# Reordering the transfers of a scratch inverse, and five half-row moves, in the plan of a two-layer RWKV-7 / differential-attention trunk on one core

## The chip, the core and the metric

The kernel runs on one core of one Trainium2 chip. The metric is device time in microseconds of one execution. A core has five instruction streams that run in order and meet only at semaphores: TensorE (PE in the profile, its weight loads PEld), VectorE (DVE), ScalarE (ACT), GpSimd (POOL) and SyncE (SP), which here issues nearly all transfers; transfers are carried out by 16 DMA engines. The three runs of the kernel before took 1398.43 to 1399.07 us, with a median of 1398.93.

## What is computed

One inference step of a two-layer trunk, for a prompt of 512 tokens and a sample of 32 tokens, which the kernel treats as one matrix of 544 columns. Layer 0 is RWKV-7 time mixing, layer 1 differential attention; each has one input projection, cross attention to a memory, a SiLU gate, one output projection and a residual. The recurrence of layer 0, per head and token, is

```python
def step(S, inp):
    r_t, k_t, v_t, w_t, kk_t, a_t = inp
    sa = jnp.einsum('bhvk,bhk->bhv', S, -kk_t)
    S = (S * w_t[:, :, None, :] + sa[..., None] * (kk_t * a_t)[:, :, None, :]
         + v_t[..., None] * k_t[:, :, None, :])
    return S, jnp.einsum('bhvk,bhk->bhv', S, r_t)
...
y = (y - mean) * lax.rsqrt(var + GN_EPS) * ln_w + ln_b      # per head
y = y + jnp.sum(r * k * r_k, axis=-1, keepdims=True) * v
out = jnp.concatenate([y_mix, y_mem], axis=-1) * jax.nn.silu(gate)
return x + out @ w_out, S_T, last_row
```

There are 24 heads of 64; all matrices are float32.

## The kernel before

Layer 0 takes the heads two at a time: twelve *pairs*, each 128 partitions wide. The tokens are cut into eight chunks of 64, and the sample makes a ninth of 32. Inside a chunk the recurrence is solved as a triangular system, so a pair needs, for each of its chunks, small matrices (tile `at`, and `ats` for the sample) and the inverse of their triangular parts. The parts of the work on one pair are Python generators, and each step of one is a few instructions:

- `prep` (`rw_prep`, 33 steps) makes decays, keys and the small matrices of a pair, and near its end writes the triangular parts to a scratch in DRAM, `sc1` (the profile shows `sc<-at` x4 and `sc<-ats`).
- `inv` (`rw_invert`) reads `sc1` back in another layout into the tile `m` (`m<-sc` x6), and GpSimd eliminates: 31 times a product `tm<-u,m` (L867) and a sum `u<-u,tm` (L869).
- `back` (`rw_back`) writes the result `u` to another scratch, `sc2` (`sc<-u` x6), and `at` (`rw_at`) reads it from there into `at` and `ats` (`at<-sc` x4, `ats<-sc`).
- `mrg` (`rw_merge`) joins the two halves of the inverses: VectorE transposes (`t1b<-at`), TensorE multiplies (`ps_w`), ScalarE copies (`wm`, `at<-ps_w`).
- `val`, `chain` and `out` are the recurrence itself: nine chunks one after another (`ps_c`, `avz`, `sv`, `sd`, `SB`), then the outputs (`ps_yc`, `yt<-ps_yc`). `smp` is the sample's chunk and state.
- `fin` (`rw_finish`) is the norm of a pair's output: sums (`gs`), squares on ScalarE (`gsq`), `rsq`, a root by a chain of small VectorE instructions (`nt`, `q`), the product `yt<-yt,q`, transposes on TensorE (`ps_y`), and the gate.

The body of layer 0 is one loop over the pairs. Its turn for pair `pr` walks the 23 rows of the table `PLAN`: each row begins with one step of the chain of pair `pr`, and has two halves, each a list of steps (kind, pair relative to `pr`, and two costs in us that say how much TensorE and VectorE work the step is taken for). Between the steps matmuls of the main stream (`ps_g`, the projections) are laid, as many as the costs leave room for. While pair `pr` runs its chain, `prep` works on pairs `pr`+1 to `pr`+3, `inv` begins the inverse of pair `pr`+2, and `back`, `at` and `mrg` bring in the one of pair `pr`+1. Each engine's order is the program's order; no scheduler changes it.

The weights of the stream come in blocks: each block is loaded in two halves (`raw`, five buffers), two blocks ahead, split into a high part by ScalarE (`whi<-raw`) and a low part by VectorE (`wlo<-raw,whi`), and used in three products. The split's instructions, the gates and the token shift (`raw<-ps_g`, `shc`, `rkv<-raw`, `raw<-PC`, then VectorE's `rkv<-raw,PA,rkv`) are put off and let in one at a time at the end of a half row (`some`), where the costs have left room. Every transfer of this stretch is issued by SP, in program order, and SP stands at a transfer until what it waits for is there. Nearly every instruction goes through a recording helper, so its line is L106.

Of the kernel before, what the change touches and what calls it, by code (L numbers as in the profile page):

```python
# [47 lines left out]
FULL = ("full", 0, 0, 0)  # L48
PLAN = [
    [[("val", 0, 0.95, 0), ("prep", 2, 0.1, 0)], [("prep", 2, 0, 0.42)]],  # L50
    [[], [("prep", 2, 0, 1.04)]],
    [[("prep", 1, 0.53, 0)], [("prep", 1, 0, 0), ("prep", 2, 0.56, 1.0)]],
    [[("prep", 2, 0, 0)], [("prep", 2, 0, 1.0)]],
    [[("smp", 0, 0.11, 0.28), ("prep", 1, 0.4, 0)], [("prep", 2, 0, 0.86)]],
# [1 line left out]
    [[("prep", 2, 0, 1.1), ("smp", 0, 0.21, 0.29)], [("prep", 2, 0, 0.86)]],  # L56
    [[("prep", 2, 1.1, 1.37)], []],
    [[("smp", 0, 0.21, 0)], [("prep", 2, 0, 0.9)]],
    [[("prep", 2, 1.1, 1.37)], [("back", 1, 0, 0)]],
    [[("smp", 0, 0.6, 0.85)], []],  # L60
    [[("prep", 2, 0.5, 0.58)], [("at", 1, 0, 0), ("fin", -1, 0, 1.0)]],
    [[("prep", 2, 0.36, 0.43)], [("inv", 2, 0, 0), ("fin", -1, 0, 0.84)]],
    [[("prep", 2, 0.36, 0.43)], [("fin", -1, 0, 0), ("prep", 3, 0, 0)]],
    [[("prep", 2, 0.25, 0)], [("fin", -1, 0, 0.98)]],
    [[("prep", 2, 0.4, 0), ("smp", 0, 0.11, 0)], [("prep", 3, 0, 0.6)]],
    [[("prep", 3, 0.53, 0)], [("mrg", 1, 0, 0.86)]],
    [[("prep", 3, 0.11, 0.17), ("mrg", 1, 0.9, 0)], [("rsq", 0, 0, 1.5)]],
    [[("prep", 3, 0.33, 0)], [("fin", -1, 0, 0.88)]],
    [[("prep", 3, 0.33, 0)], [("prep", 3, 0, 0.1), ("fin", -1, 0.6, 1.0)]],
    [[("prep", 3, 0.33, 0)], [("mrg", 1, 0.9, 0), ("prep", 3, 0.33, 0), ("fin", -1, 0, 0.73)]],  # L70
    [[("prep", 3, 0, 1.45), ("val", 1, 0.45, 0)], [("prep", 3, 0, 0.5)]],
    [[("out", 0, 1.6, 0.7)], [("prep", 3, 0, 0)]]]
MEMPE = 4.8
SHIFTED, KEPT = 13, 24
LAM = 5
# [2173 lines left out]
```

## Time and profile before

| | before |
|---|---|
| median of 3 runs | 1398.93 us (1398.43 to 1399.07) |
| the profiled execution's own time | 1399.31 us |
| its span, first to last instruction | 1397.4 us |
| mean granted TensorE clock | 0.997 |
| TensorE busy | 1359.2 us (97%) |
| VectorE, ScalarE, GpSimd busy | 934.9, 827.4, 374.9 us |

The span is 1.9 us shorter than the execution's time; the rest lies around it. Busy times are sums over stages with different limits, so a stage is read by its own window; matmuls overlap, and a busy TensorE is one that has a matmul in flight. Rows of a timeline give start, duration, engine, line, operation and tiles, and in brackets the idle time of the engine before it and what ended that; "q" after an engine's name is its sequencer, which issues transfers. In names, an arrow separates what is written from what is read.

### The profile page before, as it was taken

To read this page: it belongs to the slowest core of one execution; us is meant where nothing else is said; L and a number is where in the kernel's file an instruction comes from. 1 tells how busy PE (TensorE), PEld (TensorE's weight loads), DVE (VectorE), ACT (ScalarE), POOL (GpSimd) and SP (SyncE) were. 2 spreads that over 40 slices of the span, in tenths; PEclk is the share of its full clock that TensorE was granted. 3 is DMA by queue.
4 is the path that set the end of the run, shared out by engine and by line. 5 is a ranking of instruction groups with operands and counts; after the bars stand their busy time and mean duration, and the time that the engine had idled before them with its cause. 6 is when DMAs were issued, how large, how long until landed. Compare 5 with 4: busy or idle time off the path is not lost.

```text
span 1397.4 us, 31954 instructions
## 1 busy us (share of the span) xinstructions
PE 1359.2 (97%) x11893; PEld 1295.8 (93%) x11893; DVE 934.9 (67%) x2345; ACT 827.4 (59%) x2304; POOL 374.9 (27%) x841
## 2 busy tenths in 40 slices
PE   8999999999999999999999999999999999999997
PEld 7988899999899998888899999999999999999997
DVE  5776778778877877676753477666466756767443
ACT  5766767867687777555543366664466546665222
POOL 2138557655775567510000040000000001001000
PEclk9999999999999999999999999999999999999999
DMA  6443222333223322342464473333333322332321
GB/s 221 149 129 83 62 59 64 91 89 76 69 77 84 77 68 69 96 119 74 128 189 130 118 217 100 92 97 90 99 92 99 99 73 84 101 105 82 91 76 72
DMA packets 264036, 139.45 MB, mean 100 GB/s; under 512 B 57721, under 2 KB 252802, under 8 KB 263882
## 3 DMA queue, kind: packets, MB, share of 16 engines
q1 hardware_dynamic: 263818, 137.41, 35.1%
q8 instruction: 94, 1.54, 0.5%
q14 instruction: 60, 0.49, 0.1%
q10 hardware_dynamic: 64, 0.02, 0.0%
HBM read 111.12 MB, written 22.91 MB: 96 GB/s over the span
## 4 chain that ended last, share of the span: by engine, by line
PE 82%; DVE 8%; ACT 5%; issue 2%; DMA 1%; POOL 1%; SPq 0%; DVEq 0%; POOLq 0%; ACTq 0%
PE ps_g L106 58%; PE ps_c L106 4%; PE ps_s L106 2%; PE ps_o L106 2%; PE ps_at L106 2%; DVE wlo L106 1%; PE ps_v L106 1%; PE ps_mo L106 1%; PE ps_mm L106 1%; PE ps_aT L106 1%; PE ps_w L106 1%; PE ps_yc L106 1%; PE ps_q L106 1%; PE ps_kv L106 1%; PE ps_mt L106 1%
## 5 line engine op out<-in xcount | busy, mean ns | idle before, releaser
L106 PE MATMUL ps_g<-hh,whi 128*128 128x272 f32 x1808 | 540.8, 300 | 0.4 <-DVE memk L106 0.2
L106 PE MATMUL ps_g<-hh,wlo 128*128 128x272 f32 x1808 | 536.0, 297 | 1.6 <-DVE wlo L106 1.6
L106 PE MATMUL ps_g<-hl,whi 128*128 128x272 f32 x1808 | 532.1, 295 | 0.6 <-DVE hl L106 0.3
L106 PEld LDWEIGHTS ps_g<-hh,wlo 128*128 128x128 f32 x1808 | 341.7, 189 | 6.3 <-DVE wlo L106 2.3
L106 PEld LDWEIGHTS ps_g<-hh,whi 128*128 128x128 f32 x1808 | 341.7, 189 | 5.7 <-DVE og L106 0.6
L106 PEld LDWEIGHTS ps_g<-hl,whi 128*128 128x128 f32 x1808 | 341.6, 189 | 4.6 <-DVE hl L106 1.3
L106 DVE TENSOR_TENSOR wlo<-raw,whi 128x512 fp32r<-128x512 f32 x314 | 220.1, 712 | 121.6 <-ACT whi L106 117.9
L106 ACT CAST whi<-raw 128x512 fp32r<-128x512 f32 x314 | 189.0, 619 | 107.8 <-PE ps_g L106 61.3
L867 POOL TENSOR_TENSOR tm<-u,m 102x84 f32<-102x84 f32 (+23 forms) x341 | 143.2, 420 | 165.7 <-DMA m<-sc 139.9
L869 POOL TENSOR_TENSOR u<-u,tm 102x84 f32<-102x84 f32 (+23 forms) x341 | 149.8, 439 | 26.6
L106 PE MATMUL ps_g<-hi,whi 128*128 128x272 f32 x512 | 149.0, 291 | 0.0
L106 PE MATMUL ps_g<-hi,wlo 128*128 128x272 f32 x512 | 147.6, 288 | 0.5 <-DVE wlo L106 0.5
L106 PE MATMUL ps_g<-lo,whi 128*128 128x272 f32 x512 | 147.5, 288 | 0.0
L1339 POOL TENSOR_TENSOR lo<-og,hi 128x544 fp32r<-128x544 f32 x8 | 13.2, 1652 | 359.9 <-ACT hi L106 359.4
L106 PEld LDWEIGHTS ps_g<-hi,wlo 128*128 128x128 f32 x512 | 96.5, 188 | 0.8 <-DVE wlo L106 0.7
L106 PEld LDWEIGHTS ps_g<-lo,whi 128*128 128x128 f32 x512 | 96.6, 189 | 0.0
L106 PEld LDWEIGHTS ps_g<-hi,whi 128*128 128x128 f32 x512 | 96.5, 189 | 0.0
L106 ACT ACTIVATE pt<-ps_s,snm 128x128 f32<-128x128 f32 (+3 forms) x96 | 50.9, 531 | 41.7 <-DVE snm L106 41.6
L106 DVE SCALAR_TENSOR_TENSOR SB<-ps_c,dl,sd 64x64 f32<-64x64 f32 x168 | 47.3, 282 | 38.9 <-PE ps_c L106 35.7
L1766 POOL TENSOR_TENSOR hl<-hn,hh 128x544 fp32r<-128x544 f32 x8 | 12.5, 1565 | 211.9 <-ACT hh L106 211.8
L106 ACT COPY sv<-ps_c 64x64 f32<-64x64 f32 x192 | 39.3, 205 | 33.0 <-PE ps_c L106 30.8
L106 ACT ACTIVATE sg<-ps_g 128x272 f32<-128x272 f32 x64 | 25.3, 395 | 54.5 <-PE ps_g L106 49.2
(402 smaller groups left out, 2580.6 us busy)
## 6 DMA issues: line engine op xcount, KB each, us to landing
raw<-in_rw_in_dram SPq DMA_DIRECT2D x114, 256.0 KB
raw<-in_df_in_dram SPq DMA_DIRECT2D x112, 256.0 KB
raw<-in_w_out_dram SPq DMA_DIRECT2D x64, 256.0 KB
oscr<-sg SPq DMA_DIRECT2D x16, 272.0 KB
lo<-oscr SPq DMA_DIRECT2D x16, 272.0 KB
m<-sc SPq DMA_DIRECT2D x33, 128.0 KB
raw<-in_w_mem_v_dram SPq DMA_DIRECT2D x16, 256.0 KB
kh<-kh SPq DMA_DIRECT2D x24, 136.0 KB
```

The source lines that it names most:

```text
L106: return lambda *a, **k: self.trunk.tie(self, issue(*a, **k))
L867: nc.gpsimd.tensor_tensor(tm[:, :n, :wd], u3[:, :n, kx : kx + 1].to_broadcast(sh), m3[:, kx : kx + 1, kx + 1 :].to_broadcast(sh), ALU.mult)
L869: nc.gpsimd.tensor_tensor(u3[:, :n, kx + 1 :], u3[:, :n, kx + 1 :], tm[:, :n, :wd], ALU.add)
L1339: (self.nc.gpsimd if g % 2 and self.o1 else self.ve).tensor_tensor(lo[:], t, hi[:].bitcast(F32), ALU.subtract)
L1766: nc.gpsimd.tensor_tensor(self.hl[:, k, :], h[:], self.hh[:, k, :].bitcast(F32), ALU.subtract)
```

## The change

The table `PLAN` is rewritten; nothing else is touched. `back` moves from row 9 to row 11 and `inv` from row 12 to row 11, behind it; `at` moves from row 11 to row 12. The writes of `sc1` belong to the `prep` step in the first half of row 11, which stays, so that the transfers of a turn now come in the order: next matrices written, results written, matrices read, results read. Five other steps move by half a row: `prep` of row 1 and `fin` of rows 13 and 18 to the first half, `prep` of row 15 to the second half, and `out` from the first half of row 22 to the second half of row 21.

```diff
-    [[], [("prep", 2, 0, 1.04)]],
+    [[("prep", 2, 0, 1.04)], []],
...
-    [[("prep", 2, 1.1, 1.37)], [("back", 1, 0, 0)]],
+    [[("prep", 2, 1.1, 1.37)], []],
     [[("smp", 0, 0.6, 0.85)], []],
-    [[("prep", 2, 0.5, 0.58)], [("at", 1, 0, 0), ("fin", -1, 0, 1.0)]],
-    [[("prep", 2, 0.36, 0.43)], [("inv", 2, 0, 0), ("fin", -1, 0, 0.84)]],
-    [[("prep", 2, 0.36, 0.43)], [("fin", -1, 0, 0), ("prep", 3, 0, 0)]],
+    [[("prep", 2, 0.5, 0.58)], [("fin", -1, 0, 1.0), ("back", 1, 0, 0), ("inv", 2, 0, 0)]],
+    [[("prep", 2, 0.36, 0.43), ("at", 1, 0, 0)], [("fin", -1, 0, 0.84)]],
+    [[("prep", 2, 0.36, 0.43), ("fin", -1, 0, 0)], [("prep", 3, 0, 0)]],
     [[("prep", 2, 0.25, 0)], [("fin", -1, 0, 0.98)]],
-    [[("prep", 2, 0.4, 0), ("smp", 0, 0.11, 0)], [("prep", 3, 0, 0.6)]],
+    [[("smp", 0, 0.11, 0)], [("prep", 2, 0.4, 0), ("prep", 3, 0, 0.6)]],
...
-    [[("prep", 3, 0.33, 0)], [("fin", -1, 0, 0.88)]],
+    [[("prep", 3, 0.33, 0), ("fin", -1, 0, 0.88)], []],
...
-    [[("prep", 3, 0, 1.45), ("val", 1, 0.45, 0)], [("prep", 3, 0, 0.5)]],
-    [[("out", 0, 1.6, 0.7)], [("prep", 3, 0, 0)]]]
+    [[("prep", 3, 0, 1.45), ("val", 1, 0.45, 0)], [("prep", 3, 0, 0.5), ("out", 0, 1.6, 0.7)]],
+    [[], [("prep", 3, 0, 0)]]]
```

On SP, in the turn of pair 3, where pair 4's results come back and pair 5's inverse begins, the rows before are these (`u_3747` is pair 4's result, `at_1695` and `sc_4458` are pair 5's matrices and their scratch, `at_90` is where pair 4's results go):

```order
 L106 DMA raw<-in_rw_in_dram 128x4x128 x2
 L106 DMA sc_4408<-u_3747 32x11x32 x2
 L106 DMA sc_4408<-u_3747 32x10x32
 L106 DMA sc_4409<-u_3747 2x11x32 x2
 L106 DMA sc_4409<-u_3747 2x10x32
 L106 DMA raw<-in_rw_in_dram 128x4x128 x2
 L106 DMA sc_4458<-at_1695 32x8x32 x4
 L106 DMA sc_4458<-ats 32x2x32
 L106 DMA at_90<-sc_4408 32x8x32 x4
 L106 DMA ats<-sc_4409 32x2x32
 L106 DMA m_4495<-sc_4458 32x1024
```

and now these (the names' numbers are new, the tiles the same):

```order
 L106 DMA raw<-in_rw_in_dram 128x4x128 x4
 L106 DMA sc_4450<-at_1695 32x8x32 x4
 L106 DMA sc_4450<-ats 32x2x32
 L106 DMA sc_4463<-u_3723 32x11x32 x2
 L106 DMA sc_4463<-u_3723 32x10x32
 L106 DMA sc_4464<-u_3723 2x11x32 x2
 L106 DMA sc_4464<-u_3723 2x10x32
 L106 DMA m_4471<-sc_4450 32x1024
...
 L106 DMA at_90<-sc_4463 32x8x32 x4
 L106 DMA ats<-sc_4464 32x2x32
```

Both weight loads and the writes of pair 5's matrices now stand ahead of the transfer that waits for GpSimd's result, and the reads of pair 4's results stand behind the six reads of pair 5's matrices.

On VectorE, in rows 16 to 18 of the same turn (merge, root and product of the norm), the rows before are:

```order
 L106 STREAM_TRANSPOSE t1b<-at_90 32x256 x2
 L106 TENSOR_TENSOR avz<-ps_c,avz 64x128
 L106 TENSOR_SCALAR q_99<-ps_s_4695 128x16
 L106 SCALAR_TENSOR_TENSOR rkv<-raw_485,PA,rkv 128x544
...
 L106 TENSOR_TENSOR wlo<-raw,whi 128x512
 L106 TENSOR_TENSOR yt_1689<-yt_1689,q_100 128x640
 L106 SCALAR_TENSOR_TENSOR SB_540<-ps_c,dl,sd 64x64 x2
 L106 TENSOR_TENSOR wlo<-raw,whi 128x512
```

and now:

```order
 L106 STREAM_TRANSPOSE t1b<-at_90 32x256 x2
 L106 SCALAR_TENSOR_TENSOR rkv<-raw_485,PA,rkv 128x544
 L106 TENSOR_TENSOR avz<-ps_c,avz 64x128
 L106 TENSOR_SCALAR q_99<-ps_s_4697 128x16
...
 L106 TENSOR_TENSOR yt_1689<-yt_1689,q_100 128x640
 L106 TENSOR_TENSOR wlo<-raw,whi 128x512
 L106 SCALAR_TENSOR_TENSOR SB_540<-ps_c,dl,sd 64x64 x2
```

The token shift's `rkv` moves ahead of `avz`, and the product `yt` ahead of the `wlo` that stood before it; the second `wlo` moves further down. The chain of the root, left out here, is the same in both.

On ScalarE, in rows 15 to 17 of that turn, the copies stood like this (`s_4674` is the copy that the transpose `ps_s` reads):

```order
 L106 COPY bt<-ps_bt 128x512
 L106 COPY so<-ps_so 64x64 x2
 L106 COPY raw_485<-ps_g 128x272
 L106 COPY s_4674<-ps_ss 128x128
 L106 COPY shc<-raw_485 128x2
 L106 ACTIVATE rkv<-raw_485,dv 128x544
 L106 COPY raw_485<-PC 128x1
```

and now stand like this:

```order
 L106 COPY so<-ps_so 64x64 x2
 L106 COPY raw_485<-ps_g 128x272
 L106 COPY bt<-ps_bt 128x512
 L106 COPY shc<-raw_485 128x2
 L106 ACTIVATE rkv<-raw_485,dv 128x544
 L106 COPY raw_485<-PC 128x1
 L106 COPY s_4678<-ps_ss 128x128
```

`bt` moves behind the evacuation of the main stream, and `s` behind the token shift's three instructions.

## The prediction

> **What bounds the kernel now.** I read the page's totals first, then a table by stage, then who waits for whom, then the timelines of one turn of the loop over head pairs.
>
> ```profile
> span 1397.4 us, 31954 instructions
> PE 1359.2 (97%) x11893; PEld 1295.8 (93%) x11893; DVE 934.9 (67%) x2345; ACT 827.4 (59%) x2304; POOL 374.9 (27%) x841
> 143.00:200.00 57.00, 54.58 (x544) 49.76 (x543) 43.08 (x108) 38.60 (x116) 35.80 (x87) 1.00 0.21 51
> 290.00:336.00 46.00, 45.14 (x470) 42.26 (x469) 36.62 (x91) 33.44 (x97) 29.23 (x65) 1.00 0.32 83
> 520.00:575.00 55.00, 50.25 (x526) 46.67 (x524) 43.84 (x115) 38.05 (x112) 30.05 (x70) 0.99 0.32 79
> ```
>
> The last three rows are stages of the pair loop (window, its length, busy time of PE, PEld, DVE, ACT, POOL). TensorE is the bound at full granted clock (1.00): in a middle turn it idles 46.00 - 45.14 = 0.86 us, in the first stage 2.42, in the one where the weight stream thins out 4.75. The edit leaves every TensorE instruction in place and only reorders them, so all that it can win is such idle time, and it loses only by making new. These waits end it:
>
> ```profile
> PE ps_y L106 <- DVE yt L106: 5.7, 9, 1.0
> PE ps_c L106 <- DVE avz L106: 2.4, 4, 1.4
> PE ps_w L106 <- DVE t1b L106: 2.1, 4, 1.1
> PE ps_ss L106 <- ACT bt L106: 0.8, 2, 0.6
>   PE ps_y L106: 5.0, 7
> ```
>
> (Four rows of the waits: total us, times, longest; the last is from the view of tile yt between 200 and 575 us.) The recurring one is ps_y, the transposes of the normalised output: seven waits, 5.0 us, one in each steady turn; two more, 0.7 us, come after 575.
>
> **The reordered transfers.** SP in the turn whose inverses are pair 4's (read back) and pair 5's (begun), and GpSimd beside it:
>
> ```profile
> 276.76 0.98 SPq L106 DMA_DIRECT2D raw<-in_rw_in_dram  x2
> 286.30 2.35 SPq L106 DMA_DIRECT2D sc<-u  x6
> 288.75 0.94 SPq L106 DMA_DIRECT2D raw<-in_rw_in_dram  x2
> 289.79 1.93 SPq L106 DMA_DIRECT2D sc<-at  x4
> 291.81 0.40 SPq L106 DMA_DIRECT2D sc<-ats  x1
> 292.31 1.85 SPq L106 DMA_DIRECT2D at<-sc  x4
> 294.75 2.04 SPq L106 DMA_DIRECT2D m<-sc  x6
> 286.04 0.23 POOL L869 TENSOR_TENSOR u<-u,tm 102x11 f32<-102x11 f32 x1
> 298.95 0.24 POOL L867 TENSOR_TENSOR tm<-u,m 102x31 f32<-102x31 f32 x1 [8.77 <-DMA m<-sc]
> SPq L106 <- POOL u L869: 68.5, 9, 10.2
> ```
>
> SP runs in order. It stands at the results' write (sc<-u) until the elimination ends (286.27): 68.5 us in nine turns, with the next weight load behind it. That load then goes out at 288.75, directly ahead of the matrices' writes (sc<-at). GpSimd starts 298.95 - (294.75 + 2.04) = 2.16 us after the last read of m was issued.
>
> In the new order both weight loads, then sc<-at and sc<-ats, come before anything that waits for GpSimd. What holds the chain then is VectorE's mask of the sample chunk:
>
> ```profile
> 282.18 0.67 DVE L106 TENSOR_TENSOR wlo<-raw,whi 128x512 fp32r<-128x512 f32 x1
> 284.65 1.29 DVE L106 TENSOR_TENSOR at<-ps_at,mk 128x512 f32<-128x512 f32 x2 [1.79 <-PE ps_at L106]
> 288.84 0.49 DVE L106 TENSOR_TENSOR ats<-ps_ats,mk 128x128 f32<-128x128 f32 x2
> 126.35 1.78 SPq L106 DMA_DIRECT2D at<-sc  x4
> 129.10 0.43 DVE L106 STREAM_TRANSPOSE t1b<-at 32x256 f32<-32x256 f32 x1 [0.60 <-DMA at<-sc]
> ```
>
> The second load needs a fifth raw buffer, free at 282.85 when that wlo ends; at is complete at 285.94, so the four sc<-at go out at 286; ats is complete at 289.33. Then, with the rows' durations and 0.1 us between kinds: sc<-ats to 289.8; six sc<-u to 292.2 (GpSimd was done at 286.3, so SP does not stand); six m<-sc to 294.3; four at<-sc to 296.2. GpSimd starts at 294.3 + 2.16 = 296.5, which is 2.5 us earlier. That gains nothing by itself, since no row above has TensorE waiting for GpSimd. The price is on the results: before they were issued by 294.16, now by 296.2. The first turn shows a released reader 129.10 - (126.35 + 1.78) = 0.97 us after the last issue; behind m's reads I bound it by m's own 2.16. So at lands between 297.2 and 298.4. Who waits:
>
> ```profile
> 297.87 0.58 DVE L106 SCALAR_TENSOR_TENSOR SB<-ps_c,dl,sd 64x64 f32<-64x64 f32 x2 [1.83 <-PE ps_c L106]
> 298.37 0.89 DVE L106 STREAM_TRANSPOSE t1b<-at 32x256 f32<-32x256 f32 x2
> 299.74 0.29 DVE L106 TENSOR_TENSOR avz<-ps_c,avz 64x128 f32<-64x128 f32 x1 [0.48 <-PE ps_c L106]
> 300.27 0.79 DVE L106 SCALAR_TENSOR_TENSOR rkv<-raw,PA,rkv 128x544 f32<-128x544 f32 x1
> 302.91 0.77 DVE L106 TENSOR_TENSOR wlo<-raw,whi 128x512 fp32r<-128x512 f32 x1
> 303.60 0.89 DVE L106 TENSOR_TENSOR yt<-yt,q 128x640 f32<-128x640 f32 x1
> 299.74 0.69 PE L106 MATMUL ps_w<-t1b,at 32*32 32x32 f32 x32
> 304.64 0.63 PE L106 MATMUL ps_y<-ident,yt 128*128 128x128 f32 x4 [0.68 <-DVE yt L106]
> L106 SPq DMA_DIRECT2D at<-sc x48: 307/441/1572, 126.4 to 607.9; - x48
> ```
>
> t1b, the merge's transpose, starts at 298.37, held by TensorE's ps_c, not by data: the results arrive 0 to 1.2 us ahead of it. If they are late, avz, the root chain and yt queue behind t1b on VectorE; ps_w has 299.74 - 299.26 = 0.48 us of cover. I take no stall in a normal turn, and +1.0 us in all for turns where one issue on SP is slow: the last row (min, median, max ns) has an issue of 1.57 against 0.44, 1.13 more, of which 0.5 is covered; one or two of nine turns. Bounds 0 and, with every turn late, the rival below.
>
> The Trainium skill, "DMA: Bandwidth & Descriptors", section "Anatomy of one DMA", fits a DMA (on GpSimd's path) as about 2.0 us fixed plus its bytes; from the issue of the last 32 KB read (296.2 - 0.44) that would be an estimated landing at 297.8, so no allowance, and a sum 1.0 us lower. The first turn's row gives 0.97 + 0.44 = 1.4 us for the same kind of read with nothing ahead of it, so here the rows are the shorter and decide.
>
> **The five moved half steps.** (1) `fin` in row 18: the multiply yt now stands before one wlo (0.77) instead of behind it, and rkv (0.79) moves ahead of avz, into the 0.48 us that VectorE idled there. So yt starts 0.7 (start to start, 303.60 - 302.91) plus about 0.4 earlier, 302.5 for 303.60, and ends at 303.4; TensorE reaches ps_y at 304.64 - 0.68 = 303.96. The longest ps_y wait is 1.0, less than the 1.1 won. Take all: -5.0 - 0.7 = **-5.7**. Bound: 0, if rkv itself waits. The second wlo, now behind avz, delays nothing that a row shows waiting.
>
> (2) `prep` in row 1: zr goes ahead of rkv. Where this mattered:
>
> ```profile
> 542.80 0.58 DVE L106 TENSOR_SCALAR SB<-ps_c,dl 64x64 f32<-64x64 f32 x2 [1.39 <-PE ps_c L106]
> 544.55 0.79 DVE L106 SCALAR_TENSOR_TENSOR rkv<-raw,PA,rkv 128x544 f32<-128x544 f32 x1 [1.17 <-ACT raw L106]
> 545.25 1.11 DVE L106 TENSOR_TENSOR zr<-rkv,de 128x512 f32<-128x512 f32 x2
> 546.40 0.28 DVE L106 TENSOR_TENSOR avz<-ps_c,avz 64x128 f32<-64x128 f32 x1
> ```
>
> VectorE idles 1.17 us before rkv, and avz behind it costs TensorE the 1.4 us wait. zr (1.11) fits into that gap: **-1.1**, bounds 0 and -1.4.
>
> (3) `prep` in row 15 and `fin` in row 13 reorder ScalarE: bt goes behind the output copies (so) and the evacuation, and s moves behind shc, rkv and raw:
>
> ```profile
> 298.27 0.28 ACT L106 COPY s<-ps_ss 128x128 f32<-128x128 f32 x1
> 299.32 0.19 ACT L106 COPY raw<-PC 128x1 f32<-128x1 f32 x1
> 299.54 0.27 PE L106 MATMUL ps_s<-ident,s 128*128 128x128 f32 x1
> ```
>
> s, last of the same copies, ends about where raw ended, 299.51, instead of 298.55, and ps_s wants it at 299.54: the cover of 1.0 us is used up. gsq, now ahead of an evacuation that ScalarE waited for, should win some back. **+0.5** for eight turns, bounds 0 and +4 (0.5 us each). (4) `out` in row 21: ps_yc and seven ps_g change places; the same matmuls, nothing.
>
> Sum, from the profiled execution's 1399.31: -5.7 - 1.1 + 1.0 + 0.5 = -5.3, 1394.0. That execution is 0.38 above the median of the runs (1398.93), so **1393.6**.
>
> **The rivals.** A, *the results come too late.* They now queue behind the reads of m. Landing 1.6 us after t1b's turn, with 0.5 covered, costs nine turns x 1.1 = 9.9 us at ps_w, in place of the allowance: 1393.6 - 1.0 + 9.9 = 1402.5. It is slower than before by 0.2% from (5.3 + 1.0 + 2.8) / 9 = 1.0 us a turn, that is reads landing 1.5 us behind t1b's turn, at 299.9, 3.7 us after their last issue. Against it: 0.97 and 2.16 in the rows. For it: margins of about half a microsecond, and one weight load that would still have to clear the queue if its buffer came later than 282.85. The same page, section "Latency and other measured facts", has a loaded memory access at up to 2 us against 0.2; by that rule A would come true if m's reads load the memory enough. No row here shows a read that late.
>
> B, *the won time is eaten.* ps_s waits 0.5 a turn for s (+4.0 instead of +0.5) and zr wins nothing: 1393.6 + 3.5 + 1.1 = 1398.2. For it: the cover of s shrinks from 1.0 to about 0. Against it: ScalarE is 59% busy, and idles close by.
>
> C, *more than ps_y goes.* The stages 143 to 200 and 520 to 575 idle 2.4 and 4.75 us with VectorE's and ScalarE's backlog ending most waits; if about 4 more of these 7 vanish, since bt no longer sits ahead of ps_ss and VectorE catches up: 1389.5.
>
> D, *the writes do not move* (the second load waits for a later wlo): then the reordering is idle, and (1) to (3) stand: as forecast, and counted there.
>
> **How the numbers follow.** Forecast 0.55, B 0.23, A 0.12, C 0.10. A measurement of this kernel tells about 0.2%, 2.8 us, from no change: 1396.1 and 1401.7. Faster: 0.50 of the forecast and C, 0.60. Within: the forecast's 0.05, B, a little of A, 0.29. Slower: A, 0.11. The forecast's own range is 1391.5 to 1396.5; for 8 in 10 it must take in B and half of C: 1389.0 to 1400.0.
>
> **What would show it.** Right: ps_y gone from the waits; GpSimd's first tm 2 to 3 us earlier against t1b; SP without a wait for u. Wrong: ps_w waiting for t1b in every turn, with t1b waiting for at<-sc (A); a new row ps_s for ACT s (B); ps_y still there with yt started late because rkv waited for raw.

## The result and the profile after

The changed kernel takes 1384.87 us (median of four runs, 1382.06 to 1385.84) against 1399.0 for the kernel before: a ratio of 0.9895, with a 95% interval of 0.9878 to 0.9912. It is 14.1 us faster, 2.7 times the 5.3 us of the forecast's sum, and lies below the predicted range (1389.0 to 1400.0). The traces compared below are of executions of 1399.31 and 1382.06 us, so the one of after is 2.8 us below its median, and the traces show 17 us where the medians differ by 14.

The page of the changed kernel begins:

```profile
span 1380.3 us, 31985 instructions
PE 1352.6 (98%) x11893; PEld 1292.9 (94%) x11893; DVE 931.4 (67%) x2345; ACT 828.0 (60%) x2304; POOL 384.7 (28%) x841
```

TensorE has the same 11893 matmuls, and is busy 6.6 us less with them. For the steady part I cut both traces at the end of VectorE's mask of the sample chunk (`ats`), from pair 3's mask to pair 11's, eight turns. First the window of the kernel before, then, of the changed one, the same eight turns, its first stage, one middle turn and the last stage (length, then busy time of PE, PEld, DVE, ACT, POOL):

```profile
197.46:562.78 365.32, 356.02 (x3694) 332.35 (x3693) 290.35 (x722) 263.69 (x762) 232.34 (x513) 1.00 0.30 78
```

```profile
196.49:549.62 353.13, 351.27 (x3694) 331.87 (x3693) 286.45 (x723) 264.28 (x762) 240.06 (x512) 1.00 0.31 78
...
143.00:200.00 57.00, 54.94 (x547) 50.30 (x546) 42.86 (x110) 39.32 (x118) 36.94 (x87) 1.00 0.26 62
285.30:329.84 44.54, 44.54 (x469) 42.16 (x468) 35.82 (x92) 33.40 (x96) 30.93 (x64) 1.00 0.31 79
520.00:575.00 55.00, 52.03 (x583) 48.10 (x582) 40.51 (x105) 37.18 (x108) 39.62 (x92) 1.00 0.27 73
```

Eight turns with the same 3694 matmuls take 353.13 instead of 365.32 us, 45.7 a turn before and 44.1 now. Of these 12.2 us the idle time gives 9.30 - 1.86 = 7.4, and 4.8 come out of time that was shown as busy. In the middle turn TensorE has no idle time left at all. Four of the waits that end TensorE's idle time are now (total us, times, longest; before, their totals were 1.5, 2.1, 5.7 and 2.4):

```profile
PE ps_c L106 <- ACT yt L106: 2.3, 6, 0.6
PE ps_w L106 <- DVE t1b L106: 1.1, 3, 0.6
PE ps_y L106 <- DVE yt L106: 0.7, 2, 0.4
PE ps_c L106 <- DVE avz L106: 0.3, 1, 0.3
```

The seven waits of the steady turns at ps_y are gone; the two late ones (0.7) are still there. Of the four waits behind avz one is left: the 1.4 us one is down to 0.3. The waits behind ScalarE's yt grew a little. In the changed kernel, SP and GpSimd in the turn that the prediction showed:

```profile
282.15 1.81 SPq L106 DMA_DIRECT2D sc<-at  x4
285.33 0.30 SPq L106 DMA_DIRECT2D sc<-ats  x1
285.73 2.38 SPq L106 DMA_DIRECT2D sc<-u  x6
288.16 2.41 SPq L106 DMA_DIRECT2D m<-sc  x6
290.67 1.79 SPq L106 DMA_DIRECT2D at<-sc  x4
```

```profile
281.02 0.23 POOL L869 TENSOR_TENSOR u<-u,tm 102x11 f32<-102x11 f32 x1
281.20 1.34 POOL L787 TENSOR_TENSOR rkk<-rkv 128x544 f32<-128x544 f32 x1
292.48 0.24 POOL L867 TENSOR_TENSOR tm<-u,m 102x31 f32<-102x31 f32 x1 [2.48 <-DMA m<-sc]
```

The elimination ends at 281.25 and SP asks for its result only at 285.73: SP no longer waits for GpSimd's result, but for VectorE's mask. VectorE, a little later in the turn:

```profile
293.79 0.58 DVE L106 SCALAR_TENSOR_TENSOR SB<-ps_c,dl,sd 64x64 f32<-64x64 f32 x2 [1.61 <-PE ps_c L106]
294.28 0.89 DVE L106 STREAM_TRANSPOSE t1b<-at 32x256 f32<-32x256 f32 x2
295.22 0.79 DVE L106 SCALAR_TENSOR_TENSOR rkv<-raw,PA,rkv 128x544 f32<-128x544 f32 x1
296.04 0.29 DVE L106 TENSOR_TENSOR avz<-ps_c,avz 64x128 f32<-64x128 f32 x1
...
298.67 0.83 DVE L106 TENSOR_TENSOR yt<-yt,q 128x640 f32<-128x640 f32 x1
```

There is no wait in front of t1b: the results, whose last read was issued by 292.46, were there. GpSimd's first tm starts 1.8 us ahead of t1b, where it was 0.6 behind it: 2.4 us earlier, as forecast (2.5). And rkv, avz, the root and yt follow without a gap.

### The profile page after: what moved, and what is told of

The parts are those of the page before. It is cut to its first block, busy times and chain, and to the rows that moved or that the text cites. A ratio compares the mean times of both kernels' runs of the same rounds, so it can differ in the third digit from the quotient of the medians.

```text
span 1380.3 us, 31985 instructions
## 1 busy us (share of the span) xinstructions
PE 1352.6 (98%) x11893; PEld 1292.9 (94%) x11893; DVE 931.4 (67%) x2345; ACT 828.0 (60%) x2304; POOL 384.7 (28%) x841
## 4 chain that ended last, share of the span: by engine, by line
PE 88%; DVE 6%; ACT 3%; issue 1%; DMA 1%; SPq 0%; DVEq 0%; ACTq 0%
PE ps_g L106 62%; PE ps_c L106 5%; PE ps_s L106 2%; PE ps_o L106 2%; PE ps_at L106 2%; PE ps_v L106 2%; PE ps_mo L106 1%; PE ps_mm L106 1%; PE ps_w L106 1%; PE ps_wa L106 1%; DVE wlo L106 1%; PE ps_aT L106 1%; PE ps_yc L106 1%; PE ps_kv L106 1%; PE ps_q L106 1%
## 5 line engine op out<-in xcount | busy, mean ns | idle before, releaser
L867 POOL TENSOR_TENSOR tm<-u,m 102x84 f32<-102x84 f32 (+23 forms) x341 | 146.1, 429 | 100.6 <-DMA m<-sc 71.7
L869 POOL TENSOR_TENSOR u<-u,tm 102x84 f32<-102x84 f32 (+23 forms) x341 | 155.8, 457 | 26.6
```

What stands on the lines that cost most here:

```text
L867: nc.gpsimd.tensor_tensor(tm[:, :n, :wd], u3[:, :n, kx : kx + 1].to_broadcast(sh), m3[:, kx : kx + 1, kx + 1 :].to_broadcast(sh), ALU.mult)
L869: nc.gpsimd.tensor_tensor(u3[:, :n, kx + 1 :], u3[:, :n, kx + 1 :], tm[:, :n, :wd], ALU.add)
```

## The experiments

The kernel before was timed beside each group of four: 1398.58, 1398.62 and 1399.19 us. Differences are taken against the one beside, or against the 1384.87 of the changed kernel, whose four runs (1382.06 to 1385.84) belong to none of these groups; so a difference of a microsecond or two against it is rough.

**The two halves of the change.** First the transfers alone:

```diff
-    [[("prep", 2, 1.1, 1.37)], [("back", 1, 0, 0)]],
+    [[("prep", 2, 1.1, 1.37)], []],
...
-    [[("prep", 2, 0.5, 0.58)], [("at", 1, 0, 0), ("fin", -1, 0, 1.0)]],
-    [[("prep", 2, 0.36, 0.43)], [("inv", 2, 0, 0), ("fin", -1, 0, 0.84)]],
+    [[("prep", 2, 0.5, 0.58)], [("fin", -1, 0, 1.0), ("back", 1, 0, 0), ("inv", 2, 0, 0)]],
+    [[("prep", 2, 0.36, 0.43), ("at", 1, 0, 0)], [("fin", -1, 0, 0.84)]],
```

> The three transfer steps alone (the five half-row moves undone). Theory S (the stops): TensorE never waited for GpSimd or for SP, so the order of the transfers is worth nothing to it; 1399 us, within 1 us of the kernel before, though SP's waits for GpSimd's result vanish and GpSimd starts about 2.5 us earlier. Rival T (the transfers): with SP no longer standing at the results' write, weight halves and inverses arrive earlier, the backlog on VectorE and ScalarE shrinks and several small stops with it: 1391 to 1394 us, a third to a half of the 14.1 us.

Measured: 1397.35 us, a ratio of 0.9992 (0.9984 to 1.0001): 1.2 us, not told apart from nothing. That is theory S but for 0.2 us, and rival T falls; SP's waits for GpSimd's result went away and next to nothing came of it.

Then the five half-row moves alone, with the transfers in their old places:

```diff
-    [[], [("prep", 2, 0, 1.04)]],
+    [[("prep", 2, 0, 1.04)], []],
...
-    [[("prep", 2, 0.36, 0.43)], [("fin", -1, 0, 0), ("prep", 3, 0, 0)]],
+    [[("prep", 2, 0.36, 0.43), ("fin", -1, 0, 0)], [("prep", 3, 0, 0)]],
...
-    [[("prep", 2, 0.4, 0), ("smp", 0, 0.11, 0)], [("prep", 3, 0, 0.6)]],
+    [[("smp", 0, 0.11, 0)], [("prep", 2, 0.4, 0), ("prep", 3, 0, 0.6)]],
...
-    [[("prep", 3, 0.33, 0)], [("fin", -1, 0, 0.88)]],
+    [[("prep", 3, 0.33, 0), ("fin", -1, 0, 0.88)], []],
...
-    [[("out", 0, 1.6, 0.7)], [("prep", 3, 0, 0)]]]
+    [[], [("prep", 3, 0, 0)]]]
```

(`out` goes to the end of the row above.)

> The five half-row moves alone, transfers in their old order. Theory S: all of the gain is here, 1385 us (within 1.5). Rival T: 1390 to 1393 us, since what the transfers bring is missing. If the two only work together, 1395 or more.

Measured: 1400.19 us, 1.0008 (0.9999 to 1.0016). Theory S falls, and T with it; the third case of the expectation holds, that the two only work together: the halves give -1.2 and +1.6 and together -14.1. The trace, of its fastest run (1397.54 us), says why. Its waits, and its eight turns in the same cut as above:

```profile
PE ps_q L106 <- POOL rkk L787: 13.8, 8, 2.7
...
PE ps_y L106 <- DVE yt L106: 0.4, 1, 0.4
PE ps_c L106 <- DVE avz L106: 0.3, 1, 0.3
```

```profile
196.73:563.15 366.42, 352.71 (x3694) 332.25 (x3693) 290.54 (x722) 264.70 (x762) 235.64 (x508) 1.00 0.30 77
```

The stops at ps_y and avz are gone as in the changed kernel, and TensorE's busy time is nearly that of the changed kernel (352.71 and 351.27). But the eight turns are as long as before, with 13.7 us of idle time, and a wait that was not there takes it: ps_q, for GpSimd's product rkk. GpSimd forms rkk right behind the elimination. In the kernel before, GpSimd in the turn of the prediction and around the next elimination, and then TensorE's use of the first rkk:

```profile
286.23 1.36 POOL L787 TENSOR_TENSOR rkk<-rkv 128x544 f32<-128x544 f32 x1
...
330.78 0.23 POOL L869 TENSOR_TENSOR u<-u,tm 102x11 f32<-102x11 f32 x1
330.97 1.34 POOL L787 TENSOR_TENSOR rkk<-rkv 128x544 f32<-128x544 f32 x1
344.63 0.24 POOL L867 TENSOR_TENSOR tm<-u,m 102x31 f32<-102x31 f32 x1 [9.27 <-DMA m<-sc]
```

```profile
289.50 0.62 PE L106 MATMUL ps_q<-rkk,hb 128*128 128x272 f32 x2
```

rkk is ready at 287.59, and TensorE takes it at 289.50: no wait, with 1.9 us to spare. But GpSimd has a loop of its own with SP: the elimination (298.95 to 331.01, 32.1 us), then results written, next matrices written, results read, next matrices read and landed (13.6 us, of which SP stands 1.5 for TensorE's ps_g), then the next elimination at 344.63. That is 45.68 us, and TensorE's turn was 45.71 (289.33 to 335.04). Single turns scatter, from 44.4 to 46.9 us between the starts of eliminations, so that this pair of turns agrees so closely is in part chance; over seven turns the means are 45.54 (209.73 to 528.49) and, from ps_q to ps_q, 45.61 (243.78 to 563.06). GpSimd was the second bound, just below the first. Take TensorE's stops away alone, and GpSimd's loop sets the turn; shorten that loop alone, and TensorE does.

The margin from rkk's end to ps_q, over the nine turns, says the same. It is 0.05 us in the first turn and 1.7 to 4.1 in the others in the kernel before, 3.5 to 6.4 with the transfers alone, 0.05 in every turn with the five moves alone, and 1.9 to 3.2 in the changed kernel. With the five moves alone the loop even became longer, 46.42 us a turn (209.18 to 534.14): its eight eliminations took 32.65 us on the mean, against 31.95 in the kernel before.

**The largest term alone.** The product yt ahead of one wlo, nothing else:

```diff
-    [[("prep", 3, 0.33, 0)], [("fin", -1, 0, 0.88)]],
+    [[("prep", 3, 0.33, 0), ("fin", -1, 0, 0.88)], []],
```

> Only the step fin of row 18 moved: yt ahead of one wlo on VectorE, TensorE's order unchanged. Counted from start to start of TensorE's matmuls, not by shown idle time, ps_y costs 6.8 us less after the change than before, where the idle rows say 5.0. Theory S: this move takes nearly all of that, 1392.2 us (within 1.5), and the ps_y waits fall from 5.7 to about 1. By the prediction on record, with idle time as the measure and rkv ahead of avz counted in: at most 5.7, 1393.3. Rival U (the product is early only if the steps before it are early too: rkv and the root's chain come ahead through the other moves): half of it, 1395 to 1397 us, with ps_y waits of 2 to 4 us left.

Measured: 1399.79 us, 1.0003 (0.9994 to 1.0013), with runs from 1395.60 to 1401.95. Its waits:

```profile
PE ps_q L106 <- POOL rkk L787: 4.6, 7, 1.3
...
PE ps_y L106 <- DVE yt L106: 0.4, 1, 0.4
```

The move takes ps_y's waits away, 5.7 to 0.4 us, more than S asked, and the time is unchanged: seven waits for rkk come in their place. All three expectations miss, since none had the stall go to GpSimd.

**`out` alone.**

```diff
-    [[("prep", 3, 0, 1.45), ("val", 1, 0.45, 0)], [("prep", 3, 0, 0.5)]],
-    [[("out", 0, 1.6, 0.7)], [("prep", 3, 0, 0)]]]
+    [[("prep", 3, 0, 1.45), ("val", 1, 0.45, 0)], [("prep", 3, 0, 0.5), ("out", 0, 1.6, 0.7)]],
+    [[], [("prep", 3, 0, 0)]]]
```

> Only the step out moved from row 22 to row 21. The prediction on record says nothing, 1399 us: the same matmuls in another order. Rival V: the move shifts where the token shift, the splits and the evacuations fall on ScalarE and VectorE for the whole turn behind it, and so takes the hidden stops at ps_c behind avz (4.4 us less from start to start after the change) and at the sample's transposes (so, si: 2.3 us less): 1392 to 1395 us.

Measured: 1395.7 us, 0.9982 (0.9973 to 0.9990): 2.9 us faster. So the move that I costed at nothing is worth something, as rival V says, a little less than it asks, and mostly not at its places: from the start of one matmul to the start of the next, ps_c behind avz costs 0.5 us more than before, and what falls is spread over ps_g (-1.2), si (-0.9, which V named), ps_c behind SB (-0.7) and smaller ones.

**The loop theory, tested on the two together.** The transfers and `fin` of row 18 (the diffs of the first and third experiment together):

> The three transfer steps and fin of row 18, the other four moves undone. Theory L (two loops): with fin of row 18 alone ps_y gave back 7.1 us from start to start, and 6.5 came back as ps_q's waits for GpSimd's rkk, because GpSimd's own loop through SP (elimination 32, then 13.3 us until the next matrices are read) was as long as a turn; the transfers alone gave 1.2. Where the transfers break that loop, the 7.1 stay: 1398.6 - 7.1 - 1.2 = 1390.3 us (within 1.5), ps_q's waits for rkk 0. Rival M (only the whole set of moves works): 1395 us or more, with the stops elsewhere, not at ps_q.

Measured: 1394.7 us, 0.9974 (0.9965 to 0.9983). No wait for rkk is left, as L says, and the transfers now let the move pay; but it pays 2.7 us beyond the transfers alone and not 7. Against the kernel before, ps_y's starts come 5.8 us cheaper; ps_c behind SB costs 2.2 more, and avz 0.5. The wlo that yt overtook still stands ahead of SB on VectorE, so SB comes no earlier, and TensorE, now sooner at the matmul that needs it, waits there: nearly half of the stop moved on to what was late next. That reading rests on VectorE's order and the start times. L's 1390.3 misses; M's 1395 or more is met but for 0.3 us, and the stops are elsewhere, as it says, not at ps_q.

**What breaks the loop.** The five moves again, with the matrices read ahead of the results, and the writes where they were before:

```diff
-    [[("prep", 2, 0.5, 0.58)], [("at", 1, 0, 0), ("fin", -1, 0, 1.0)]],
-    [[("prep", 2, 0.36, 0.43)], [("inv", 2, 0, 0), ("fin", -1, 0, 0.84)]],
+    [[("prep", 2, 0.5, 0.58)], [("inv", 2, 0, 0), ("at", 1, 0, 0), ("fin", -1, 0, 1.0)]],
+    [[("prep", 2, 0.36, 0.43)], [("fin", -1, 0, 0.84)]],
```

(against the five moves alone)

> The five moves with the writes in their old places, SP standing at the results' write as before; only inv is put ahead of at, so that the next matrices are read before the results. Theory L: GpSimd's loop loses the five transfers in front (at<-sc and ats<-sc, 2.3 us): 46.2 - 2.3 = 43.9 us, less than TensorE's turn of 44.4, so ps_q's waits for rkk fall from 13.8 us to under 3 and the time from 1400.2 to 1385 to 1388 us. Rival W (it is SP standing at that write that costs, since weight halves are held behind it): ps_q's waits or others stay, 1395 us or more.

Measured: 1392.24 us, 0.9958 (0.9945 to 0.9970), 8.0 less than the five moves alone. There is no wait for rkk any more, by a change of order in SP's queue and nothing else, and SP still stands at the results' write for 77.9 us, so it was GpSimd's loop, and rival W falls as to the cause. But the time misses L's by 4 us. The waits of its TensorE and SP, and what ended the idle time ahead of t1b and of the matmuls that read it (190 to 600 us):

```profile
PE ps_w L106 <- DVE t1b L106: 6.0, 10, 1.8
...
SPq L106 <- POOL u L869: 77.9, 9, 9.7
...
SPq L106 <- DMA sc<-at: 15.7, 12, 2.6
...
  DMA at<-sc: 6.8, 8
```

Two things that L left out. SP now reads the matrices back directly behind their write, and stands there until the write has landed: 15.7 us in twelve waits, where the kernel before, with the results' reads in between, has one such wait of 0.7 us. And the results are read last, behind that wait, so t1b waits for them (6.8 us in eight waits, where the changed kernel has none), and TensorE for t1b, ten times. This is the prediction's rival A, in its place: 4.9 us more of idle time at ps_w than in the changed kernel (6.0 against 1.1). The changed order shows neither: the write of the results lies between the write and the read of the matrices and covers the landing, and all of it starts when the mask is done rather than when GpSimd is.

**GpSimd loaded.** The changed kernel, with rkk formed four times over instead of once:

```diff
                 spare.tensor_tensor(rkk[:], r[:], k2[:], ALU.mult)
+                if spare is not self.ve:
+                    for _ in range(3):
+                        spare.tensor_tensor(rkk[:], r[:], k2[:], ALU.mult)
```

> The changed kernel with GpSimd's product rkk formed four times instead of once in nine pairs (the same result, 3 x 1.34 = 4.0 us more on GpSimd behind the elimination). Theory L: GpSimd's margin ahead of ps_q is 1.9 to 3.2 us in the changed kernel, so ps_q waits 0.8 to 2.1 us for it; each wait also moves the next matrices and the one after has its margin back, so about every second turn: 1389 to 1394 us. Rival: GpSimd is never what TensorE waits for, here too: 1385.

Measured: 1395.7 us, 0.9981 (0.9972 to 0.9990), 10.8 more than the changed kernel.

```profile
PE ps_q L106 <- POOL rkk L790: 7.9, 5, 2.4
...
PE ps_q L106 <- DVE gs L106: 1.5, 1, 1.5
```

```profile
329.19 1.35 POOL L787 TENSOR_TENSOR rkk<-rkv 128x544 f32<-128x544 f32 x1
330.61 4.79 POOL L790 TENSOR_TENSOR rkk<-rkv 128x544 f32<-128x544 f32 x3
```

In the changed kernel itself, one turn earlier:

```profile
285.68 0.62 PE L106 MATMUL ps_q<-rkk,hb 128*128 128x272 f32 x2
```

The load, 4 to 5 us more on GpSimd a turn, brings back 7.9 + 1.5 = 9.4 us of waits at the same matmul (the one put down to gs comes 0.05 us behind rkk's end). So the margin at ps_q is real and small, 285.68 - (281.20 + 1.34) = 3.1 us in the turn shown, and it is what the transfers bought. The time is above the 1389 to 1394 expected: the three copies took up to 4.8 us rather than 4.0, and not every second turn paid but eight of nine, in which ps_q starts 0.05 us behind the last copy (six of them with idle time shown).

**The single moves, left out of the changed kernel one at a time.** The trace of the changed kernel is of its fastest run, so sums from start to start against it come out larger than the differences of the medians: the traced executions differ by 6.2 us without `fin` of row 18, 7.6 with ScalarE's old order and 4.2 without `prep` of row 1, the medians by 2.9, 4.7 and 1.0. `fin` of row 18 back in its second half:

> The changed kernel with fin of row 18 put back. Theory L: the ps_y stops return, 1384.9 + 6.8 = 1391.7 us (within 1.5), and nothing else; so fin of row 18 and the other four moves share the 14.1 about evenly. Rival M: more than 10 us return, 1395 us or more. By the prediction on record, where fin of row 18 is nearly all of it: 1397 to 1399.

Measured: 1387.78 us, so this move is worth 2.9 us and not 6.8.

```profile
PE ps_y L106 <- DVE yt L106: 3.0, 9, 0.6
```

Without it ps_y waits 3.0 us and not 5.7: the other moves bring yt forward by themselves and had taken half of the stop.

`out` back in row 22:

> The changed kernel with out put back to row 22. Beside ps_y, the changed kernel's TensorE spends from start to start 4.4 us less on ps_c behind avz, 2.1 less on ps_g and 2.3 less on so and si, and 2.7 more on ps_c behind bt. out alone gave 2.6 us of the whole. If the moves add up: 1384.9 + 2.6 = 1387.5 us (within 1). If out is what takes avz's stops too, together with the others: 1390 to 1392. By the prediction on record: 1384.9, nothing.

Measured: 1386.44 us: 1.6, nearest the first case (moves that add up) and not the prediction's nothing, though its interval (0.9901 to 0.9928) overlaps the changed kernel's (0.9878 to 0.9912).

`prep` of row 15 and `fin` of row 13 back, that is, ScalarE's old order:

```diff
-    [[("prep", 2, 0.36, 0.43), ("fin", -1, 0, 0)], [("prep", 3, 0, 0)]],
+    [[("prep", 2, 0.36, 0.43)], [("fin", -1, 0, 0), ("prep", 3, 0, 0)]],
...
-    [[("smp", 0, 0.11, 0)], [("prep", 2, 0.4, 0), ("prep", 3, 0, 0.6)]],
+    [[("prep", 2, 0.4, 0), ("smp", 0, 0.11, 0)], [("prep", 3, 0, 0.6)]],
```

> The changed kernel with prep of row 15 and fin of row 13 put back, so ScalarE's old order. Theory L with the leave-outs so far (fin of row 18 is worth 2.9 us in the changed kernel, out 1.6, and both are missing of 14.1 only in part): these two steps and prep of row 1 share the other 8 us or so. If ScalarE's order is the larger part: 1384.9 + 6 = 1391 us (within 1.5), with the stops at so behind bt and part of ps_y's back. If it is the smaller: 1387. By the prediction on record, which charged 0.5 us for it: 1384.4.

Measured: 1389.61 us: these two are worth 4.7 us, the largest share of a single part. From start to start the loss is spread: 1.4 us at so, 1.4 at ps_y, 1.3 at ps_w, 1.1 at ps_c behind SB, 0.8 at si.

Only `prep` of row 15 of the two (the second hunk alone):

> The changed kernel with only prep of row 15 put back (fin of row 13 stays): bt is copied ahead of the output copies and the evacuation again. If bt's place is what matters of ScalarE's order: the same as with both put back (within 1). If it is fin of row 13, which squares earlier: 1385 to 1386.

Measured: 1388.38 us, 3.5 of the 4.7. So the place of bt seems to matter most and `fin` of row 13 to be the rest; but the five runs reach from 1385.64 to 1388.97, and their interval (0.9901 to 0.9929) overlaps the changed kernel's, so the split is rough.

`prep` of row 1 back:

```diff
-    [[("prep", 2, 0, 1.04)], []],
+    [[], [("prep", 2, 0, 1.04)]],
```

> The changed kernel with prep of row 1 put back. By the prediction on record it is worth one stop of 1.1 us: 1386.0. Rival: it is what takes ps_c's hidden stops behind avz in every turn (3.8 us of the 4.4 from start to start): 1388.5 us (within 1), with avz's pitch back.

Measured: 1385.86 us, 1.0 us, with an interval (0.9890 to 0.9917) that overlaps the changed kernel's. The 1.4 us wait behind avz that the prediction named is back. The rival is right that avz's starts come back dearer in all (4.2 us), but ps_c behind bt gets 2.9 cheaper at the same time: the move trades one stop for another, and that the balance is the prediction's 1.1 is in part luck.

## Why the prediction was wrong

The direction was right, and so was the place of the largest idle time; the size was not.

**"That gains nothing by itself, since no row above has TensorE waiting for GpSimd."** The sentence is true (1.2 us, not told from nothing), and the conclusion that hung on it, that the transfers are a price of 1.0 us and the moves stand by themselves, is the step that failed. Taken out of the change, the transfers cost 1400.19 - 1384.87 = 15.3 us. The prediction quoted both ends of GpSimd's loop, its tm at 298.95 and SP standing for u in every turn, 68.5 us in nine, but added the terms up as if each could be had alone. A loop nearly as long as the turn, 45.54 against 45.61 us, leaves hardly a trace in the waits of the engine that is still slower by a hair: in the kernel before, one weight load of ps_q waits 0.2 us for rkk, in the first steady turn, and that is all. What was missing is the length of that loop and one subtraction, the margin at the next use (rkk ready at 287.59, used at 289.50), which the 1.5 us a turn that the change won would soon have used up.

That step had the mechanism wrong; by itself it does not make the number 8.8 us short, since the change contains both halves. The shortfall lies in the sizes of the terms below: of it, (3) makes 5.2, (4) 1.6 and the late results 1.0; (1) was 2.8 too much and (2) 0.1; 3.9 remain that the runs do not divide.

**(1) yt, -5.7.** The mechanism is as told: yt ends ahead of ps_y and the seven steady waits are gone. The two late ones, 0.7, stayed. As a term of the sum it was mis-sized: left out alone it costs 2.9, because the other moves had taken half of the same stop already; and by itself, over the transfers, it pays 2.7, because the stop moves on to SB.

**(2) zr, -1.1.** Measured -1.0, which the runs do not tell from nothing; the 1.4 us wait is down to 0.3, and avz's gain is partly ps_c's loss elsewhere.

**(3) ScalarE, +0.5.** The wrong sign, and the largest miss of the single terms: measured -4.7. I weighed s, whose cover shrinks, said that gsq should win "some" back, and gave bt's new place no price. The copy in the changed kernel, and the matmul that reads it,

```profile
295.02 0.26 ACT L106 COPY s<-ps_ss 128x128 f32<-128x128 f32 x1
295.46 0.27 PE L106 MATMUL ps_s<-ident,s 128*128 128x128 f32 x1
```

show that it ends at 295.28, 0.18 us ahead of ps_s; no ps_s waits in the steady turns: the cover held. Most of the gain, some 3.5 us, comes with the step that puts bt behind the output copies and the evacuation; by which of the small stops isn't settled.

**(4) out, nothing.** Measured -1.6, and -2.9 alone; the second is clear of the noise. "The same matmuls" is true and not enough. That their place decides when ScalarE and VectorE get their operands for the turn behind is argued from the start times, not tried.

**Late results, +1.0.** Nothing: t1b never waits for its data in the steady turns; in the one shown it starts 294.28 - 292.46 = 1.8 us behind the last issue. By the estimate from the Trainium skill's "DMA: Bandwidth & Descriptors", section "Anatomy of one DMA", no allowance was due, and none came. The risk was no fancy, though: with the matrices read first and the writes in their old places the same stall costs about 5 us.

**The measure.** "All that it can win is such idle time" failed as well: all stops were priced by idle time as shown, and that is too little. A main-stream matmul is shown with 0.29 us and the next starts 0.12 us later, so a stop has to be longer than the difference before it appears at all. At ps_y, in the changed kernel:

```profile
299.59 0.29 PE L106 MATMUL ps_g<-hh,whi 128*128 128x272 f32 x1
299.71 0.71 PE L106 MATMUL ps_y<-ident,yt 128*128 128x128 f32 x5
```

and in the kernel before:

```profile
303.68 0.28 PE L106 MATMUL ps_g<-hh,whi 128*128 128x272 f32 x1
304.64 0.74 PE L106 MATMUL ps_y<-ident,yt 128*128 128x128 f32 x5 [0.68 <-DVE yt L106]
```

From start to start that is 0.96 before and 0.12 now: the stop cost 0.84 us where 0.68 is shown. Summed so over all 60 matmuls of ps_y (start of each less the start of the one ahead, from the trace) the two executions differ by 6.8 us, and by 5.0 in idle time. Stops under 0.16 us don't show at all; 4.8 of the 12.2 us that eight turns won were such "busy" time. The Trainium skill, "Perfetto Trace Analysis", section "Identifying the Most-Contended Engine", warns that the busy share of pipelined matmuls is a poor measure of how near TensorE is to its limit; the windows here agree, with 356.02 us busy before and 351.27 after for the same 3694 matmuls.

**The rivals.** C, more than ps_y goes, was the nearest, at 1389.5; it named bt and VectorE's backlog, but looked for the gain in the first and last stage, while 12.2 of the 17 us between the traces came in the eight steady turns. A and B didn't come, though A did once its order was built. D fell: the writes moved.

**What stays open.** The single moves are worth 2.9 + 4.7 + 1.0 + 1.6 = 10.2 us when left out one at a time, and the transfers 1.2 alone, 11.4 of 14.1. The rest may be shared by moves that cover for each other; the runs don't divide it further. Why each of the small stops behind ScalarE's old order falls where it does was read from start times only, not tried.

## What to carry to other kernels

Before pricing a stop of the slowest engine, follow each other engine's own loop once around, through the queues that it waits for, and compare its length with the turn's: a loop that is shorter by nothing shows no wait, and takes back whatever is won. When two such loops are close, edits on one alone are worth nothing in either direction and the pair is worth the whole; test them together before dropping either. Price stops of pipelined matmuls from start to start, and of several moves around one stop count the gain once.

## What the runs showed of the hardware

**GpSimd is slowed by VectorE instruction by instruction.** The elimination of the turn shown took 32.06 us before and 33.66 in the changed kernel (292.48 to 326.14), with the same 62 instructions; the mean of eight is 31.95 and 32.83. The same sum, 102 x 40, in the kernel before, and with the five moves alone, with VectorE beside the latter:

```profile
284.15 0.27 POOL L869 TENSOR_TENSOR u<-u,tm 102x40 f32<-102x40 f32 x1
```

```profile
285.63 0.88 POOL L869 TENSOR_TENSOR u<-u,tm 102x40 f32<-102x40 f32 x1
```

```profile
285.70 0.67 DVE L106 TENSOR_TENSOR wlo<-raw,whi 128x512 fp32r<-128x512 f32 x1
```

It takes 0.88 instead of 0.27 us beside a wlo, and ends 0.14 us behind that wlo's end. The Trainium skill, "SBUF — State Buffer", section "Who interferes with whom", has a VectorE instruction with two inputs in SBUF contend with a GpSimd instruction that reads there, for ports that one of them holds at a time; wlo reads raw and whi, both in SBUF, and the rows agree. So GpSimd's loop can get longer by a new order of VectorE alone. It is not a matter of more VectorE work: VectorE is busy for 79.2% of the eight eliminations before and 79.3% in the changed kernel. Which instructions make the 0.9 us isn't settled.

**A read of a scratch behind its own write makes the queue stand.** With the matrices read directly behind their write SP waited up to 2.6 us for the landing of its write, in order, with everything behind it held; six other transfers in between (2.38 us of issue in the changed kernel) hide that.
